# Two-layer hybrid decoder trunk: new order of the SBUF pools, slots of 2048 bytes, moving sides and weights 64 bytes apart modulo 128

## The chip, the core and the metric

The kernel runs on one core of a Trainium2 chip. The metric is the device time of one execution in microseconds (us), the median of three runs. The engines are named as in the profile: PE (matmuls), PEld (the weight loads of the same engine), DVE, ACT, POOL, and SP, whose queue issues nearly all DMAs.

## What is computed

The reference is a trunk of two layers over 256 positions of width 1024. Each layer has four token mixers that read one common projection, a gated merge, a SwiGLU of width 2816 and a gated side input; the rest is norms and residual adds. Nearly all of its arithmetic is products of a weight matrix with the activations:

```python
for i in range(DEPTH):                       # 2 layers
    u = _rmsnorm(h, norm_mix[i]) @ w_in[i]   # columns go to four mixers
    ...                                      # NSA, HGRN2, retention, RWKV-7, each to 256 columns
    merged = sum(sigmoid(x @ w_gate[i, m] + b_gate[i, m]) * (y[m] @ w_branch[i, m]) for m in range(4))
    h = h + merged @ w_out[i]
    x = _rmsnorm(h, norm_ffn[i])
    h = h + (silu(x @ w_ffn_gate[i]) * (x @ w_ffn_up[i])) @ w_ffn_down[i]
    x = _rmsnorm(h, norm_ple[i])
    h = h + sigmoid(x @ w_ple_gate[i]) * (p[i] @ w_ple_proj[i])
```

## The kernel before, in words

Activations stand feature-major: 128 partitions by 256 positions for each of the 8 pieces of the width. Every product is made in three matmuls of rounded fp32 ("fp32r"): weights and activations are each split into a rounded part (`hi`, tiles wh, xh) and the rest (`lo`, tiles wl, xl), and `mm3` (L221 to L223) adds wl·xh, wh·xl and wh·xh into one PSUM tile. The weights are the stationary side (128x128, loaded anew for each matmul), the activations the moving side (128x256). `gemm_pair` does the same where the last pieces of the activations come late (L256 to L258). `in_tm1` and `in_tm2` (L425 to L427) have the sides exchanged.

Weights come in tiles of 128x1024. `w_load` issues the DMA on SP into wr (4 buffers), ACT rounds it into wh (L206, 3 buffers), DVE or POOL subtracts into wl (L207, 3 buffers). One tile feeds 24 matmuls. A scheduler with priorities sets the order on each engine; small matmuls of the mixers (L141) are put between those of the big products.

The moving sides are: xh and xl, the normed activations (all of the projection, the gates, the SwiGLU's gate and up products); tiles A, T and Y made by `split` (L370, L371); U and M for the side input's gate. They come from the rotating tags A (18 buffers), B (13), U, T (6 each), Y0 to Y3 (2 each), M (4), which `t` and `g` take out of one pool.

SBUF is laid out by the pools in the order const, act, w, and inside a pool by first use. A tile's size in bytes for one partition is rounded up to 32. Some slots of A and U are larger than 2048 bytes (`rwkv_in` asks for T + 1 columns, 2056 bytes, `rwkv` for 65 where there are 64, `nsa_cmp` for 528), so their neighbours start at different places. The built program's addresses for one partition, modulo 128 (plain arithmetic on the layout, no times):

| tile | role | before | changed |
|---|---|---|---|
| wh, wl (all buffers; slices of a tile are 512 bytes apart) | weights | 64 | 64 |
| xh, xl (pieces are 1024 bytes apart) | moving | 64 | 0 |
| A | moving in the output and down products | 64, 96, 0, 32 in turn | 0 |
| U | moving in the side input's gate | 0 and 64 in turn | 0 |
| M | moving there, too | 64 | 0 |
| T | moving in the last pieces of the down product | 32 | 0 |
| Y0, Y3 | moving in two of the branch products | 0 | 0 |
| Y1, Y2 | moving in the other two, and for p | 32 | 0 |

`small` (vectors and small weights) is loaded into one tile for each layer, sm[0] and sm[1], both near the start. `rwkv` and `nsa_hid` read the small weights out of it.

Of the kernel before, what the change touches and what calls it, by code (L numbers as in the profile page):

```python
# [23 lines left out]
F32 = mybir.dt.float32  # L24
F32R = mybir.dt.float32r
BF = mybir.dt.bfloat16
I32 = mybir.dt.int32
AF = mybir.ActivationFunctionType
OP = mybir.AluOpType
# [3 lines left out]
P = 128  # L33
L = 2
T = 256
# [9 lines left out]
NV = 96  # L45

S_VEC = 0
S_WAU, S_GUP, S_K2, S_V2, S_PK, S_PV = (NV + x for x in (0, 256, 512, 640, 704, 720))
NS = S_PV + 16


C_ID, C_COS, C_SIN, C_DEC = 0, 128, 384, 640
# [98 lines left out]
class Trunk:  # L151
# [4 lines left out]

    def t(self, shape, tag, dt=F32, bufs=1):
        self.n += 1
        return self.act.tile(list(shape), dt, tag=tag, name=f"{tag}_{self.n}", bufs=bufs)

    def g(self, shape, stream=None, dt=F32):

# [8 lines left out]
    def run(self):  # L171
        tc = self.tc
        self.n = 0
        with (
            tc.tile_pool(name="const", bufs=1) as self.cst,
            tc.tile_pool(name="act", bufs=1) as self.act,
            tc.tile_pool(name="w", bufs=1) as self.wp,
            tc.tile_pool(name="ps", bufs=1, space=PS) as self.psp,
        ):
            self.body()  # L180
# [248 lines left out]
    def in_tm2(self, l):  # L429

        nc = self.nc
        ps = [self.ps([P, 512], "mm") for _ in range(2)]
        xs = self.xs()
        for g in range(2):
            hi, lo = self.w_load(self.ins["w_tm2"][l, g])
            for kk in range(4):
                k = 4 * g + kk
                s = slice(kk * 256, (kk + 1) * 256)
                for c in range(2):
                    ts = slice(c * P, (c + 1) * P)  # L440
                    self.mm3x(ps[c][:, :256], xs[k][0][:, ts], xs[k][1][:, ts], hi[:, s], lo[:, s], k == 0, k == 7)
        tm = self.t([P, 2, T], "tm2")
        for c in range(2):
            nc.vector.tensor_scalar(tm[:, c], ps[c][:, :256], self.rt[:, c:c + 1], 0.5, op0=OP.mult, op1=OP.mult)
        return tm
# [41 lines left out]
    def rwkv_in(self, l):  # L487
        nc = self.nc
        V = nc.vector
        v = lambda col: self.vec[l][:, col:col + 1]  # L490
        self.stream = "A"
        if l == 0:
            self.one_less_mu(l)
        ums = []
        for p in (3, 1, 0, 2):
            u = self.g([P, 2, T + 1])
            nc.gpsimd.memset(u[:, :, 0:1], 0.0)
            ps = self.in_pair(l, 2 * p, 2 if p == 3 else 0, "pA" if p in (3, 1) else "mm")
            mul = V.tensor_mul(u[:, :, 1:], ps, self.rstd_b)
            if p == 1:  # L500
                self.second = mul
            w = self.g([P, 2, T])
            um = self.g([P, 2, T])
            for c in range(2):
                i = 2 * p + c
                nc.scalar.activation(w[:, c], u[:, c, 1:], AF.Copy, scale=self.ommu[l][:, i:i + 1])
                V.scalar_tensor_tensor(um[:, c], u[:, c, :T], v(V_MU + i), w[:, c], op0=OP.mult, op1=OP.add)
            ums.append(um)
        return ums

    def rwkv(self, l, ums):
# [30 lines left out]
        V.tensor_tensor_scan(b.rearrange("p j t -> p (j t)"), self.reset, lw.rearrange("p j t -> p (j t)"), 0.0,  # L542
                             op0=OP.mult, op1=OP.add)
        b4 = b.rearrange("p j (c t) -> p j c t", c=4)
        pt = self.g([P, 2, 4, 65])
        nc.gpsimd.memset(pt[:, :, :, 0:1], 1.0)
        for j in range(2):
            nc.scalar.activation(pt[:, j, :, 1:], b4[:, j], AF.Exp)
# [354 lines left out]
    def nsa_in(self, l):  # L903
        nc = self.nc
        V = nc.vector
        sm = self.sm[l]
        rb = self.rstd
        lo, up = slice(0, 64), slice(64, 128)
        ps = self.in_pair(l, 16)
        kv = self.g([P, 16, 2, 16], "U")  # L910
        for i, src in ((0, lo), (1, up)):
            kb = kv[:, :, i].rearrange("p j n -> p n j")
            jn = lambda x: x.rearrange("p (n j) -> p n j", j=16)
            V.tensor_mul(kb[lo, :15], jn(ps[src, 0, :240]), jn(rb[src, :240]))
            V.tensor_mul(kb[up, :15], jn(ps[src, 0, 16:]), jn(rb[src, 16:]))
            V.tensor_copy(kv[:, :, i, 15], sm[:, S_PK + 16 * i:S_PK + 16 * i + 16])

        ksw = self.g([P, 528], "U")
        kx = ksw[:, 16:].rearrange("p (x b t) -> p b x t", x=2, b=2)
        xt = lambda a: a.rearrange("p (x t) -> p x t", x=2)  # L920
        for i, (src, dst) in enumerate(((lo, up), (up, lo))):
            V.tensor_mul(kx[src, i], xt(ps[src, 1]), xt(rb[src]))
            nc.scalar.activation(kx[dst, i], kx[src, i], AF.Copy)
        q = self.g([P, 2, T], "U")
        ps = self.in_pair(l, 14)
        V.scalar_tensor_tensor(q, ps, 0.125, self.rstd_b, op0=OP.mult, op1=OP.mult)
        return kv, ksw, q
# [138 lines left out]
    def setup(self):  # L1066
        nc, cst = self.nc, self.cst
        self.inv_dm = cst.tile([P, 1], F32, name="inv_dm")
        nc.vector.memset(self.inv_dm, 1.0 / DM)
        w = cst.tile([P, 1], F32, name="first")  # L1070
        nc.scalar.activation(w, self.inv_dm, AF.Copy)

        z = cst.tile([P, P], BF, name="zeros")
        nc.vector.memset(z, 0.0)
        ps = self.ps([P, P], "mm")
        for _ in range(72):
            nc.tensor.matmul(ps, z, z, start=True, stop=True)
        self.c = c = cst.tile([P, NC_], F32, name="cst")
        self.h = cst.tile([P, 8, T], F32, name="h")
        self.sm = [cst.tile([P, NS], F32, name=f"sm{l}") for l in range(L)]  # L1080
        nc.scalar.dma_start(self.sm[0][:, :NV], self.ins["small"][0][:, :NV])
        self.ahead = []
        for p in range(3):
            nc.sync.dma_start(self.h[:, 2 * p:2 * p + 2], self.ins["x"][:, 2 * p:2 * p + 2])
            if p == 0:
                self.ahead.append(self.w_tiles([self.ins["w_fm"][0, 6]], 2))
        nc.scalar.dma_start(c[:, :P], self.ins["consts"][:, :P])
        self.vec = [s[:, S_VEC:S_VEC + NV] for s in self.sm]
        self.xh = cst.tile([P, 8, T], F32R, name="xh")
        self.xl = cst.tile([P, 8, T], F32R, name="xl")  # L1090
        self.ident = c[:, C_ID:C_ID + P]
        self.ommu = [cst.tile([P, 8], F32, name=f"ommu{l}") for l in range(L)]

# [13 lines left out]
    def one_less_mu(self, l):  # L1107
        self.nc.vector.tensor_scalar(self.ommu[l], self.vec[l][:, V_MU:V_MU + 8], -1.0, 1.0, op0=OP.mult, op1=OP.add)

    def setup_late(self):  # L1110
        nc, cst, c = self.nc, self.cst, self.c
        with self.tc.issue_after(self.last_load.ins):
            nc.sync.dma_start(self.sm[0][:, NV:], self.ins["small"][0][:, NV:])
            nc.sync.dma_start(c[:, P:], self.ins["consts"][:, P:NC_])
            nc.sync.dma_start(self.sm[1], self.ins["small"][1])
        self.cos, self.sin = c[:, C_COS:C_COS + T], c[:, C_SIN:C_SIN + T]
        self.dec = c[:, C_DEC:C_DEC + 1024].rearrange("p (h b t) -> p h b t", h=4, b=2)
        self.rmask = c[:, C_RM:C_RM + 256]
# [123 lines left out]
    def layer(self, l):  # L1242
# [11 lines left out]
        with lane("A", "G"):  # L1254
            if l == 0:
                self.setup_late()
        with lane("A", "G"):
            self.tc.cur_priority += (30, 60)[l]
            y3 = self.rwkv(l, ums)
# [122 lines left out]
def layouts(i):  # L1382
# [5 lines left out]
    w = A["w_in"]  # L1388
# [24 lines left out]
    sm = np.zeros((L, P, NS), np.float32)  # L1413
    cv = lambda a: a.reshape(-1, P).T
    for l in range(L):
        sm[l, :64, S_WAU:S_WAU + 256] = A["rwkv_w_up"][l]
        sm[l, 64:, S_WAU:S_WAU + 256] = A["rwkv_a_up"][l]
        sm[l, :, S_GUP:S_GUP + 256] = A["rwkv_g_up"][l]
        sm[l, :, S_K2:S_K2 + 64] = A["nsa_cmp_k2"][l]
        sm[l, :, S_K2 + 64:S_K2 + 128] = A["nsa_cmp_k2"][l]  # L1420
        sm[l, :, S_V2:S_V2 + 64] = A["nsa_cmp_v2"][l]
        for col, n in ((S_PK, "nsa_pos_k"), (S_PV, "nsa_pos_v")):
            sm[l, :64, col:col + 16] = A[n][l, :16].T
            sm[l, 64:, col:col + 16] = A[n][l, 16:].T
        vcols = ((V_MIX, "norm_mix"), (V_FFN, "norm_ffn"), (V_PLE, "norm_ple"), (V_HN, "hgrn_norm"), (V_RG, "ret_norm_g"),
                 (V_RB, "ret_norm_b"), (V_MU, "rwkv_mu"), (V_W0, "rwkv_w0"), (V_A0, "rwkv_a0"), (V_KK, "rwkv_k_k"),
                 (V_KA, "rwkv_k_a"), (V_RK, "rwkv_r_k"), (V_NG, "rwkv_norm_g"), (V_NB, "rwkv_norm_b"), (V_BG, "b_gate"))
        for col, n in vcols:
            a = cv(A[n][l].reshape(-1))
            sm[l, :, S_VEC + col:S_VEC + col + a.shape[1]] = a  # L1430
        a = cv(A["hgrn_lb_logits"].reshape(-1))
        sm[l, :, S_VEC + V_LB:S_VEC + V_LB + 4] = a
        sm[l, :, S_VEC + V_NF:S_VEC + V_NF + 8] = cv(A["norm_final"])
# [20 lines left out]
```

## Time and profile before

| what | value |
|---|---|
| median of 3 runs | 1062.36 us (1062.13 to 1063.89) |
| the profiled execution: its time | 1062.78 us |
| the profiled execution: span of its instructions | 1060.1 us |
| mean granted TensorE clock | 0.993 |
| busy: PE / PEld / DVE / ACT / POOL | 98 / 95 / 70 / 51 / 22 % |
| DMA | 171.32 MB, 162 GB/s over the span |

A matmul's record is longer than its distance to the next: matmuls are pipelined, and the records overlap. What one matmul costs in a full stream is therefore read from start to start in the timeline, or as a window's length over the matmuls that start in it; the mean duration in a group's row is not that. The time lies 2.7 us above the span (launch and end), which the change does not touch.

### The profile page before, as it was taken

The page shows a single profiled execution, that of the slowest core. Times are in us where ns is not written, and L with a number is a line of the kernel's source. Part 1 is how long each engine was busy: PE and PEld are TensorE (multiplying, and loading weights), DVE is VectorE, ACT ScalarE, POOL GpSimd, SP SyncE. Part 2 cuts the span into 40 slices and gives each one's busy share as a digit, 9 for nine tenths or more (in the row PEclk, how much of TensorE's full clock was granted, in tenths as well). Part 3 has the DMA queues.
Part 4 walks back from the last instruction along what each step waited for, and adds up shares of the span by engine and source line. Part 5 has one row for each costly group of instructions (what it writes and reads, how often), then busy time and mean ns, then how long its engine had stood idle before and what let it go on. Part 6 is the DMA issues. An engine that isn't in the chain of part 4 may idle for free.

```text
span 1060.1 us, 22813 instructions
## 1 busy us (share of the span) xinstructions
PE 1042.2 (98%) x9520; PEld 1001.9 (95%) x9520; DVE 739.5 (70%) x1216; ACT 541.8 (51%) x863; POOL 238.4 (22%) x162
## 2 busy tenths in 40 slices
PE   8999999999999999999899999999999999999996
PEld 8989988899999999999899999888999999999996
DVE  6888968755676667554878989576567767665456
ACT  5644555555655454444555545555546554444444
POOL 0100000044442242232510000000544432232322
PEclk9999999999999999999999999999999999999997
DMA  8555323255665656666544553323665656666551
GB/s 294 198 183 160 94 91 117 78 162 178 191 187 174 195 181 182 183 184 191 170 146 127 177 174 95 110 81 100 180 193 176 189 170 185 196 177 192 174 183 49
DMA packets 50359, 171.32 MB, mean 162 GB/s; under 512 B 5713, under 2 KB 6481, under 8 KB 50129
## 3 DMA queue, kind: packets, MB, share of 16 engines
q1 hardware_dynamic: 49968, 169.76, 52.1%
q8 instruction: 74, 1.21, 0.5%
q14 instruction: 29, 0.23, 0.1%
q10 hardware_dynamic: 288, 0.11, 0.0%
HBM read 168.80 MB, written 1.05 MB: 160 GB/s over the span
## 4 chain that ended last, share of the span: by engine, by line
PE 87%; DVE 7%; ACT 2%; issue 2%; POOL 1%; DMA 1%; DVEq 0%; ACTq 0%; POOLq 0%
PE mm L221 21%; PE mm L223 21%; PE mm L222 21%; PE pB L141 6%; PE pA L141 5%; DVE wl L207 2%; PE pA L221 2%; PE pA L222 2%; PE pA L223 2%; PE pA L257 1%; PE pA L256 1%; PE pA L258 1%; ACT wh L206 1%; PE mm L427 1%; DVE T L1346 1%
## 5 line engine op out<-in xcount | busy, mean ns | idle before, releaser
L206 ACT ACTIVATE wh<-wr 128x1024 fp32r<-128x1024 f32 (+3 forms) x314 | 325.0, 1038 | 364.8 <-PE mm L223 243.3
L207 DVE TENSOR_TENSOR wl<-wr,wh 128x1024 fp32r<-128x1024 f32 (+3 forms) x259 | 326.5, 1262 | 146.8 <-ACT wh L206 143.8
L221 PE MATMUL mm<-xh,wl 128*128 128x256 f32 x1472 | 418.3, 284 | 0.5 <-POOL wl L207 0.5
L223 PE MATMUL mm<-xh,wh 128*128 128x256 f32 x1472 | 416.9, 283 | 0.0
L222 PE MATMUL mm<-xl,wh 128*128 128x256 f32 x1472 | 416.9, 283 | 0.0
L221 PEld LDWEIGHTS mm<-xh,wl 128*128 128x128 f32 x1472 | 277.1, 188 | 4.2 <-issue 1.6
L223 PEld LDWEIGHTS mm<-xh,wh 128*128 128x128 f32 x1472 | 277.1, 188 | 2.7 <-issue 1.5
L222 PEld LDWEIGHTS mm<-xl,wh 128*128 128x128 f32 x1472 | 277.1, 188 | 2.7 <-issue 1.5
L207 POOL TENSOR_TENSOR wl<-wr,wh 128x1024 fp32r<-128x1024 f32 (+1 forms) x55 | 130.1, 2367 | 274.9 <-ACT wh L206 274.9
L222 PE MATMUL mm<-A,wh 128*128 128x256 f32 x332 | 93.2, 281 | 0.0
L223 PE MATMUL mm<-A,wh 128*128 128x256 f32 x332 | 93.2, 281 | 0.0
L221 PE MATMUL mm<-A,wl 128*128 128x256 f32 x332 | 93.2, 281 | 0.0
L1325 POOL TENSOR_TENSOR B<-B,B 128x512 f32<-128x512 f32 x22 | 28.3, 1288 | 155.1 <-DVE B L1323 149.2
L223 PEld LDWEIGHTS mm<-A,wh 128*128 128x128 f32 x332 | 62.6, 189 | 0.0
L222 PEld LDWEIGHTS mm<-A,wh 128*128 128x128 f32 x332 | 62.6, 189 | 0.0
L221 PEld LDWEIGHTS mm<-A,wl 128*128 128x128 f32 x332 | 62.6, 189 | 0.0
L371 DVE TENSOR_TENSOR A<-B,A 128x512 fp32r<-128x512 f32 x18 | 36.6, 2033 | 33.2 <-ACT A L370 33.2
L141 PE MATMUL pA<-A,A 64*64 64x64 f32 (+3 forms) x1008 | 49.7, 223 | 0.3
L141 PEld LDWEIGHTS pA<-A,A 64*64 64x64 f32 (+3 forms) x1008 | 41.6, 135 | 8.3 <-issue 0.8
L221 PE MATMUL mm<-Y,wl 128*128 128x256 f32 x160 | 45.2, 282 | 0.0
L222 PE MATMUL mm<-Y,wh 128*128 128x256 f32 x160 | 45.0, 281 | 0.0
L223 PE MATMUL mm<-Y,wh 128*128 128x256 f32 x160 | 44.8, 280 | 0.0
(388 smaller groups left out, 1740.4 us busy)
## 6 DMA issues: line engine op xcount, KB each, us to landing
wr<-in_w_gate_dram SPq DMA_DIRECT2D x64, 512.0 KB, 3.7
wr<-in_w_fm_dram SPq DMA_DIRECT2D x46, 512.0 KB, 3.7
wr<-in_w_fg_dram SPq DMA_DIRECT2D x44, 512.0 KB, 4.4
wr<-in_w_fu_dram SPq DMA_DIRECT2D x44, 512.0 KB, 3.7
wr<-in_w_fd_dram SPq DMA_DIRECT2D x32, 512.0 KB, 4.2
wr<-in_w_branch_dram SPq DMA_DIRECT2D x16, 512.0 KB, 4.1
wr<-in_w_out_dram SPq DMA_DIRECT2D x16, 512.0 KB, 3.7
wr<-in_w_pg_dram SPq DMA_DIRECT2D x16, 512.0 KB, 4.4
```

The lines of the kernel that those rows point to most:

```text
L141: f(*args, **kw)
L206: nc.scalar.activation(hi[:, s], raw[:, s], AF.Copy)
L207: e.tensor_sub(lo[:, s], raw[:, s], hi[:, s])
L221: mm(out, wlo, xhi, start=start, stop=False)
L222: mm(out, whi, xlo, start=False, stop=False)
L223: mm(out, whi, xhi, start=False, stop=stop)
L256: mm(ps[:, c], lo, xs[k][0], start=c == 0 and k == 0, stop=False, skip_group_check=True)
L257: mm(ps[:, c], hi, xs[k][1], start=False, stop=False, skip_group_check=True)
L258: mm(ps[:, c], hi, xs[k][0], start=False, stop=k == n - 1, skip_group_check=True)
L371: self.nc.vector.tensor_sub(lo, src, hi)
L427: mm(out, xhi, whi, start=False, stop=stop)
L1325: G.tensor_mul(up, th, up)
```

## The change

The pools are opened in the order x, big, gap, w, const, act. All rotating tags go to `big`, whose slots are all exactly 2048 bytes; xh and xl stand ahead of it, and one tile of 64 bytes in `gap` stands between it and the weights. So every moving side starts at 0 modulo 128 and every weight slice at 64 (table above). In detail, for weights minus moving side modulo 512: 128 for xh and xl before, 192 for Y0 and Y3 before, 64 for all after.

The tiles larger than 2048 bytes leave these slots: the state table `pt` and `ksw` get tiles of their own, the projection `tm2` moves the other way, into a Y0 slot, and the token shift of `rwkv_in` is written without the extra column. That drops a memset on POOL for each of its four products, and the scaled copy goes straight into um (a tile less), whose columns from 1 on get the shifted term in place. The small weights of both layers share one buffer: layer 1's are loaded when layer 1 starts.

```diff
     def t(self, shape, tag, dt=F32, bufs=1):
-        return self.act.tile(list(shape), dt, tag=tag, name=f"{tag}_{self.n}", bufs=bufs)
+        pool = self.big if tag in BUFS else self.act
+        return pool.tile(list(shape), dt, tag=tag, name=f"{tag}_{self.n}", bufs=bufs)
...
+            tc.tile_pool(name="x", bufs=1) as self.xpool,
+            tc.tile_pool(name="big", bufs=1) as self.big,
+            tc.tile_pool(name="gap", bufs=1) as self.gap,
+            tc.tile_pool(name="w", bufs=1) as self.wp,
             tc.tile_pool(name="const", bufs=1) as self.cst,
             tc.tile_pool(name="act", bufs=1) as self.act,
-            tc.tile_pool(name="w", bufs=1) as self.wp,
...
-        tm = self.t([P, 2, T], "tm2")
+        tm = self.g([P, 2, T], "Y0")
...
-            u = self.g([P, 2, T + 1])
-            nc.gpsimd.memset(u[:, :, 0:1], 0.0)
+            u = self.g([P, 2, T])
...
-            mul = V.tensor_mul(u[:, :, 1:], ps, self.rstd_b)
+            mul = V.tensor_mul(u, ps, self.rstd_b)
...
-            w = self.g([P, 2, T])
             um = self.g([P, 2, T])
...
-                nc.scalar.activation(w[:, c], u[:, c, 1:], AF.Copy, scale=self.ommu[l][:, i:i + 1])
-                V.scalar_tensor_tensor(um[:, c], u[:, c, :T], v(V_MU + i), w[:, c], op0=OP.mult, op1=OP.add)
+                nc.scalar.activation(um[:, c], u[:, c], AF.Copy, scale=self.ommu[l][:, i:i + 1])
+                V.scalar_tensor_tensor(um[:, c, 1:], u[:, c, :T - 1], v(V_MU + i), um[:, c, 1:], op0=OP.mult, op1=OP.add)
...
-        pt = self.g([P, 2, 4, 65])
+        pt = self.t([P, 2, 4, 65], "rw_pt")
...
-        ksw = self.g([P, 528], "U")
+        ksw = self.t([P, 528], "ns_ksw")
...
-        w = cst.tile([P, 1], F32, name="first")
+        w = self.gap.tile([P, 16], F32, name="first")[:, :1]
...
-        self.xh = cst.tile([P, 8, T], F32R, name="xh")
-        self.xl = cst.tile([P, 8, T], F32R, name="xl")
+        self.xh = self.xpool.tile([P, 8, T], F32R, name="xh")
+        self.xl = self.xpool.tile([P, 8, T], F32R, name="xl")
...
+    def small(self, l):
+        sm = self.t([P, NS - NV], "sm")
+        self.nc.sync.dma_start(sm, self.ins["small"][l][:, NV:])
+        self.sm.append(sm)
...
-            nc.sync.dma_start(self.sm[0][:, NV:], self.ins["small"][0][:, NV:])
+            self.small(0)
             nc.sync.dma_start(c[:, P:], self.ins["consts"][:, P:NC_])
-            nc.sync.dma_start(self.sm[1], self.ins["small"][1])
+            nc.sync.dma_start(self.vec[1], self.ins["small"][1][:, :NV])
...
             if l == 0:
                 self.setup_late()
+            else:
+                with self.tc.issue_after(self.last_load.ins):
+                    self.small(l)
```

The order of the instructions stays nearly as it was. On SP one DMA is added at the start of layer 1. These are the changed kernel's rows there: the last three weight tiles of `rwkv_in`, the new load of the small weights (sm), and the first tiles of the rotary products.

```order
L210 DMA wr_6866<-in_w_fm_dram 128x1024
L210 DMA wr_6904<-in_w_fm_dram 128x1024
L210 DMA wr_6934<-in_w_fm_dram 128x1024
L1116 DMA sm_6970<-in_small_dram 128x736
L210 DMA wr_7526<-in_w_fm_dram 128x1024
L210 DMA wr_7556<-in_w_fm_dram 128x1024
```

Before, wr_6934's counterpart is followed at once by the rotary tiles. The new row stands behind the eighth and last weight tile of `rwkv_in`.

On ACT, at the end of `rwkv_in` in layer 1, the rows of before (A are the tiles u, w and um; ommu is one minus mu):

```order
L506 ACTIVATE A_6760<-A_6696,ommu_167 128x256 x2
L206 ACTIVATE wh_7531<-wr_7530 128x1024
L391 ACTIVATE U_7525<-U_7525 128x256
L506 ACTIVATE A_6830<-A_6766,ommu_167 128x256 x2
L206 ACTIVATE wh_7561<-wr_7560 128x1024
L506 ACTIVATE A_6900<-A_6836,ommu_167 128x256 x2
L206 ACTIVATE wh_7598<-wr_7597 128x1024
L506 ACTIVATE A_6970<-A_6906,ommu_167 128x256 x2
```

and the rows of the change:

```order
L509 ACTIVATE A_6761<-A_6698,ommu_176 128x256 x2
L211 ACTIVATE wh_7527<-wr_7526 128x1024
L396 ACTIVATE U_7521<-U_7521 128x256
L509 ACTIVATE A_6829<-A_6766,ommu_176 128x256 x2
L211 ACTIVATE wh_7557<-wr_7556 128x1024
L509 ACTIVATE A_6897<-A_6834,ommu_176 128x256 x2
L211 ACTIVATE wh_7594<-wr_7593 128x1024
L509 ACTIVATE A_6965<-A_6902,ommu_176 128x256 x2
```

The rows stand in the same order; only the tile written differs (um in place of w).

## Rows read from the trace of the kernel before

**Rows 1.** The page: span, busy time and share of each engine, instructions.

```profile
span 1060.1 us, 22813 instructions
## 1 busy us (share of the span) xinstructions
PE 1042.2 (98%) x9520; PEld 1001.9 (95%) x9520; DVE 739.5 (70%) x1216; ACT 541.8 (51%) x863; POOL 238.4 (22%) x162
```

**Rows 2.** Windows of SwiGLU stages: length, busy of PE to POOL, clock, DMA.

```profile
300.00:425.00 125.00, 125.00 (x1057) 125.00 (x1056) 86.68 (x91) 61.94 (x74) 42.97 (x24) 1.00 0.60 184
820.00:945.00 125.00, 125.00 (x1057) 125.00 (x1056) 86.57 (x92) 62.31 (x74) 42.95 (x24) 1.00 0.61 185
425.00:490.00 65.00, 65.00 (x552) 65.00 (x551) 34.16 (x34) 30.98 (x37) 18.97 (x11) 1.00 0.63 187
945.00:1010.00 65.00, 65.00 (x553) 65.00 (x552) 35.24 (x35) 30.18 (x37) 17.63 (x10) 1.00 0.63 183
```

**Rows 3.** Groups by form: matmuls with moving sides xh, A, Y.

```profile
L221 PE MATMUL mm<-xh,wl 128*128 128x256 f32 x1472 | 418.3, 284 | 0.5 <-POOL wl L207 0.5
...
L222 PE MATMUL mm<-A,wh 128*128 128x256 f32 x332 | 93.2, 281 | 0.0
...
L221 PE MATMUL mm<-Y,wl 128*128 128x256 f32 x160 | 45.2, 282 | 0.0
...
L256 PE MATMUL pA<-xh,wl 128*128 128x256 f32 x64 | 18.9, 296 | 3.3 <-ACT xh L310 1.9 <-DVE wl L207 1.4
...
L221 PE MATMUL pA<-xh,wl 128*128 128x256 f32 x64 | 18.3, 286 | 1.2 <-DVE wl L207 1.2
```

**Rows 4.** Timeline of PE, branch products on Y3 and Y0: start, us, form.

```profile
248.77 0.28 PE L221 MATMUL mm<-Y,wl 128*128 128x256 f32 x1
...
254.31 0.28 PE L223 MATMUL mm<-Y,wh 128*128 128x256 f32 x1
...
770.21 0.28 PE L221 MATMUL mm<-Y,wl 128*128 128x256 f32 x1
...
775.74 0.28 PE L223 MATMUL mm<-Y,wh 128*128 128x256 f32 x1
...
799.14 0.28 PE L221 MATMUL mm<-Y,wl 128*128 128x256 f32 x1
...
804.79 0.28 PE L221 MATMUL mm<-Y,wl 128*128 128x256 f32 x1
```

**Rows 5.** DMA issues of the small weights: KB, us to landing.

```profile
sm<-in_small_dram SPq DMA_DIRECT2D x1, 416.0 KB, 7.5
sm<-in_small_dram SPq DMA_DIRECT2D x1, 368.0 KB, 4.7
```

**Rows 6.** Timeline at the start of layer 1: SP's weight loads, PE's first use of sm.

```profile
541.05 5.85 SPq L205 DMA_DIRECT2D wr<-in_w_fm_dram  x4
...
561.76 0.93 PE L141 MATMUL pA<-A,sm 64*128 64x256 f32 x6
```

**Rows 7.** Line L507, the shifted term: ns min/median/max, first and last start, who waited.

```profile
L507 DVE SCALAR_TENSOR_TENSOR A<-A,sm,A x16: 465/478/726, 27.4 to 558.7; 128x256 f32<-128x256 f32 x16
...
who waited for it (us, times):
  POOL A L546: 16.5, 2
```

**Rows 8.** PE's waits over the span: in total, times, longest.

```profile
PE pB L354 <- DVE rs_y2B L294: 2.5, 2, 1.9
PE pA L256 <- ACT xh L310: 1.9, 1, 1.9
PE pA L256 <- DVE wl L207: 1.4, 2, 0.7
```

**Rows 9.** Timeline of PE in the down product of layer 1, at 965 and 996 us.

```profile
965.01 0.29 PE L222 MATMUL mm<-A,wh 128*128 128x256 f32 x1
965.14 0.28 PE L223 MATMUL mm<-A,wh 128*128 128x256 f32 x1
965.26 0.28 PE L221 MATMUL mm<-A,wl 128*128 128x256 f32 x1
...
996.13 0.29 PE L222 MATMUL mm<-A,wh 128*128 128x256 f32 x1
996.26 0.28 PE L223 MATMUL mm<-A,wh 128*128 128x256 f32 x1
```

More of the change, by code (lines that the diff above doesn't have):

```diff
@@ L47 @@
 S_VEC = 0
-S_WAU, S_GUP, S_K2, S_V2, S_PK, S_PV = (NV + x for x in (0, 256, 512, 640, 704, 720))
-NS = S_PV + 16
+S_WAU, S_GUP, S_K2, S_V2, S_PK, S_PV = 0, 256, 512, 640, 704, 720
+NS = NV + S_PV + 16
 C_ID, C_COS, C_SIN, C_DEC = 0, 128, 384, 640
@@ L1079, in setup @@
         self.h = cst.tile([P, 8, T], F32, name="h")
-        self.sm = [cst.tile([P, NS], F32, name=f"sm{l}") for l in range(L)]
-        nc.scalar.dma_start(self.sm[0][:, :NV], self.ins["small"][0][:, :NV])
+        self.vec = [cst.tile([P, NV], F32, name=f"vec{l}") for l in range(L)]
+        self.sm = []
+        nc.scalar.dma_start(self.vec[0], self.ins["small"][0][:, :NV])
         self.ahead = []
@@ L1087, in setup @@
         nc.scalar.dma_start(c[:, :P], self.ins["consts"][:, :P])
-        self.vec = [s[:, S_VEC:S_VEC + NV] for s in self.sm]
-        self.xh = cst.tile([P, 8, T], F32R, name="xh")
-        self.xl = cst.tile([P, 8, T], F32R, name="xl")
+        self.xh = self.xpool.tile([P, 8, T], F32R, name="xh")
+        self.xl = self.xpool.tile([P, 8, T], F32R, name="xl")
         self.ident = c[:, C_ID:C_ID + P]
@@ L1415, in layouts @@
     for l in range(L):
[L1416 to L1421, printed above, removed]
+        sw = sm[l, :, NV:]
+        sw[:64, S_WAU:S_WAU + 256] = A["rwkv_w_up"][l]
+        sw[64:, S_WAU:S_WAU + 256] = A["rwkv_a_up"][l]
+        sw[:, S_GUP:S_GUP + 256] = A["rwkv_g_up"][l]
+        sw[:, S_K2:S_K2 + 64] = A["nsa_cmp_k2"][l]
+        sw[:, S_K2 + 64:S_K2 + 128] = A["nsa_cmp_k2"][l]
+        sw[:, S_V2:S_V2 + 64] = A["nsa_cmp_v2"][l]
         for col, n in ((S_PK, "nsa_pos_k"), (S_PV, "nsa_pos_v")):
-            sm[l, :64, col:col + 16] = A[n][l, :16].T
-            sm[l, 64:, col:col + 16] = A[n][l, 16:].T
+            sw[:64, col:col + 16] = A[n][l, :16].T
+            sw[64:, col:col + 16] = A[n][l, 16:].T
         vcols = ((V_MIX, "norm_mix"), (V_FFN, "norm_ffn"), (V_PLE, "norm_ple"), (V_HN, "hgrn_norm"), (V_RG, "ret_norm_g"),
```

## Prediction

> **What bounds the kernel now.** I read the page's busy times first. PE is busy for 98% of the span, its weight loads for 95%, DVE for 70% and ACT for 51% [rows 1]; what PE waits for by name is 2.5 us at most in one place [rows 8]. So the time is a stream of matmuls, and the question is how far apart they start. The mean of a group (284 ns for a matmul with moving side xh [rows 3]) does not say that, since the records overlap: 1472 matmuls of one line alone give 418.3 us of "busy" time, and there are three such lines.
>
> The windows say it [rows 2]. In the two SwiGLU stages with gate and up products PE is never idle, the clock is at its full level (1.00, that is 2.4 GHz), and 1057 matmuls have records in 125 us. A record of 0.28 us that began ahead of the window counts too, some 2.4 of them, so that 1054.6 start in it: 125 / 1054.6 = 118.5 ns from start to start. Nearly all of these have moving sides in xh and xl, at the same place modulo 128 as the weights (table in the section on the change). The same reading of the down product, where the moving sides stand at 64, 96, 0 and 32, gives 65 / 549.6 = 118.3 ns in layer 0 and 65 / 550.6 = 118.1 ns in layer 1.
>
> Before the change, there is one place in which every moving side is already 64 away from the weights: the branch products on Y3 and Y0, four runs of 48 matmuls. Three of them have rows [rows 4]: 248.77 to 254.31 are 47 distances, 117.9 ns each; 770.21 to 775.74 are 47, 117.7 ns; 799.14 to 804.79 are 48, 117.7 ns. I take 117.75 ns (two decimals in us make each of them good to about 0.2 ns). This is the trace's own sample of the changed layout, and it stands beside DVE, ACT, POOL and DMA work like any other stage.
>
> **The change part by part.** *The addresses.* 118.5 - 117.75 = 0.75 ns for a matmul whose moving side now stands at the weights' place. The xh and xl products are (1472 + 64 + 64) x 3 = 4800 matmuls [rows 3], which gives 4800 x 0.75 ns = 3.6 us. The other products, apart from the branches: the down product has 1056 matmuls, the output product 384 and the side input's gate 384 (its sides U and M stand at 0 or 64). With the mean of the down stages, 118.2 ns, they give (1056 + 384 + 384) x 0.45 ns = 0.8 us. Branch products gain nothing on Y3 and Y0 and too little to count on Y1 and Y2. All of this lies on the path, because PE has no gaps in these windows [rows 2]. Sum: 4.4 us.
>
> Both ends of this price: at the low end nothing, if the 0.75 ns belong to something else than addresses; below nothing is possible, too (last rival). At the high end a matmul cannot beat its 256 columns at the full clock, 106.7 ns, so that 11.8 ns for each of some 7200 matmuls would be 85 us. I take the value of the Y runs because nothing else in the trace has the same layout, and 47 distances in a row agree within the reading.
>
> *The small mixers' matmuls* (A with A, at 64x64) had mixed places and now have one. They are 64 columns long and alternate with waits for other engines; I put them at nothing, covered by the products that the scheduler puts between them.
>
> *The token shift.* Eight memsets on POOL go, and a tile. POOL is busy for 22% [rows 1]. ACT still makes 16 copies and DVE 16 shifted terms, of 255 columns in place of 256: 478 ns x 1/256 x 16 = 0.03 us less of DVE [rows 7]. The shifted term now reads and writes the same tile, which adds no wait, as it waited for the same copy before. Behind it, only POOL waits (16.5 us in two waits [rows 7]), for work that is not on the path. Nothing.
>
> *The load of sm.* Early, 416 KB shrink to 48 KB on SP; the load took 7.5 us to land [rows 5], but PE's waits of the whole run hold no weight DMA among the longest [rows 8], so nothing is won. At the start of layer 1, 368 KB are added behind the last weight tile of `rwkv_in`. It lands in 4.7 us by its twin in layer 0 [rows 5]. On SP the four weight loads around it go out between 541.05 and 546.9 us, and PE first reads sm at 561.76 [rows 6]: 15 us or more lie between, three landings' worth. Queued behind it are the rotary tiles, whose buffers (4 in wr) hold 4 x 24 x 118.5 ns = 11.4 us of matmuls; a load that comes 4.7 us later is still covered. The single buffer adds no wait, since layer 0 reads it last in its mixers, a whole SwiGLU before layer 1 starts. If this cover were gone, it would cost 4.7 us once; I put it at nothing.
>
> *tm2 in a Y0 slot.* The slot is next wanted when `nsa` splits its result, after `hgrn` has used tm2. Nothing.
>
> So the forecast is 1062.4 - 4.4 = 1058.0 us. The profiled execution took 1062.78 us, 0.4 us above the median, so that the same sum there gives 1058.4 us and a span of about 1055.7 us. Its own range is 1053 to 1060.2: 0.75 ns taken as 0.4 to 1.3 ns.
>
> **The rivals.** *No change, 1060.2 to 1064.5 us.* The Y runs could be even for another reason: short, with two tiles that lie next to each other. For it speaks that the difference is 0.6% and the down product, where only part of the sides stand badly, is hardly faster than the gate and up products (118.1 and 118.3 against 118.5 ns). Against it: four stages agree in the order that the addresses give. The Trainium skill has a rule that points this way: "TensorE: Matmul & The Clock Gate", Part 2, "Step-by-step", has two independent SBUF read ports for PE, one for the moving side and one for weights, so that loading the next weights takes nothing from the running matmul; by that alone no address could matter and the time would stay at 1062.4. The rows of the down product (below, 0.13 us in one fixed pair) speak against its strict form. This case also holds that the change does not do what it says, if modulo 128 is not what counts.
>
> *Far faster, under 1053 us.* If the part above 106.7 ns were all a clash of the two reads and went, the time would be 1062 - 85 = 977 us; a third of it would give 1034 us. Against it stand the Y runs, in which the sides are 64 apart already and 11 ns remain. By the skill's same page, section "Back-to-back issue gap", a warm matmul of 256 columns would be 256/2.4 + 2.5 = 109.2 ns, an estimate that would give 8.6 ns x 7200 = 62 us less; the Y runs' 117.75 ns disagree with it.
>
> *Slower, above 1064.5 us.* The offset within more than 128 bytes may count. Weights minus moving side is 192 modulo 512 in the Y runs, but 64 everywhere after the change. The trace shows that single pairs of tiles can cost more: in the down product one L222 matmul takes 0.13 us to the next where its neighbours take 0.12, at the same pair in every chunk (965.01 to 965.14, 996.13 to 996.26 [rows 9]). Its moving side stands at 64 modulo 512 from the weights, which is the new relation. If every third matmul (the L222) took those 8.5 ns more, that would be 2400 x 8.5 ns = 20 us, and 1083 us. It decides from a distance of 118.9 ns on, where the loss passes 2 us. Against it: other matmuls with the same relation take 0.12 us, and the costly pair also changes its place between two matmuls, which the new layout never does.
>
> **How the numbers follow.** Forecast 0.53, no change 0.27, far faster 0.06, slower 0.14. A measurement of this kernel can tell about 0.2%, 2.1 us, from no change, so that the forecast's own range ends there. Faster: nearly all of the forecast and the far faster case, with a little of "no change" to spare, 0.60. Same: 0.27. Slower: 0.13. The range, 1053 to 1064.5, takes in the forecast and "no change" and leaves out the far faster and the slower case, 0.2 together.
>
> **What would show it.** In the window of gate and up products: 117.75 ns, some 1064 records in 125 us in place of 1057, and the down product the same. Distances in a timeline of xh matmuls would be even, as in the Y runs. The page should show PE at 98% still, the sm load landed well before its first use, and no new wait of PE. The forecast is wrong if the stream keeps 118.5 ns, or if it goes under 117 ns, and then the Y runs were no sample of the layout. If the stream gets faster and the time does not, a wait at a stage's edge took it.

## The result, and the profile after

| | before | after |
|---|---|---|
| median of 4 runs on one chip | 1062.39 us | 1049.41 us (1047.52 to 1050.96) |
| ratio after / before | | 0.9874 [0.9854, 0.9894] |
| profiled execution: time, span | 1062.78, 1060.1 us | 1048.63, 1046.9 us |

The change makes the kernel 13.0 us (1.3%) faster. The direction was forecast; the size is three times the forecast (4.4 us) and lies outside the range. In the two profiled executions 13.2 us of the difference lie in the span; the time stands 2.7 us above the span before and 1.7 us after. The first part of the page of after, beside [rows 1], shows the same kernel with a shorter time of PE and its weight loads, and little else:

```profile
span 1046.9 us, 22801 instructions
## 1 busy us (share of the span) xinstructions
PE 1026.3 (98%) x9520; PEld 986.2 (94%) x9520; DVE 738.5 (71%) x1216; ACT 542.9 (52%) x863; POOL 240.2 (23%) x154
```

PE's busy time falls by 15.9 us for the same 9520 matmuls, that of its weight loads by 15.7 us; DVE, ACT and POOL differ from before by 1 to 2 us. The 8 instructions that POOL lost are the memsets.

The windows of the two SwiGLU stages (columns as in [rows 2]; 4 us earlier in layer 0, 10 us earlier in layer 1, since the work comes earlier):

```profile
296.00:421.00 125.00, 125.00 (x1069) 125.00 (x1067) 87.06 (x92) 63.01 (x74) 43.19 (x24) 1.00 0.62 187
810.00:935.00 125.00, 125.00 (x1069) 125.00 (x1068) 87.15 (x91) 62.96 (x74) 43.24 (x24) 1.00 0.61 188
421.00:486.00 65.00, 65.00 (x554) 65.00 (x553) 34.64 (x34) 30.87 (x37) 19.40 (x11) 1.00 0.61 184
935.00:1000.00 65.00, 65.00 (x554) 65.00 (x553) 35.27 (x34) 30.23 (x37) 19.39 (x11) 1.00 0.62 187
```

With 2.4 straddling records taken off, the first two go from 118.5 to 125 / 1066.6 = 117.2 ns, the last two to 65 / 551.6 = 117.8 ns. These windows are not pure, though: the first starts some 11 us before the SwiGLU, in the output product (moving side A, about a tenth of its matmuls), the third ahead of the down product. A window that lies wholly in the gate and up products, first of before, then of after:

```profile
330.00:400.00 70.00, 70.00 (x592) 70.00 (x591) 48.52 (x46) 34.35 (x38) 23.15 (x13) 1.00 0.60 183
330.00:400.00 70.00, 70.00 (x596) 70.00 (x596) 47.59 (x44) 34.01 (x37) 22.17 (x13) 1.00 0.62 187
```

That is 70 / (592 - 2.4) = 118.7 ns before and 70 / (596 - 2.4) = 117.9 ns after: nearly what was forecast for these products, and it can't give 13 us. The gain is elsewhere. A window inside the gates stage, first of before, then of after:

```profile
223.00:248.00 25.00, 25.00 (x213) 25.00 (x212) 13.47 (x13) 12.03 (x15) 12.99 (x7) 1.00 0.59 171
```

```profile
223.00:248.00 25.00, 25.00 (x223) 25.00 (x223) 13.81 (x15) 12.79 (x17) 11.87 (x6) 1.00 0.69 202
```

25 / (213 - 2.4) = 118.7 ns there becomes 25 / (223 - 2.4) = 113.3 ns, at the same granted clock of 1.00. The timeline of PE in after shows that these are two ways in which one and the same stream can run. First in the gates stage, then in the SwiGLU, both on xh and xl:

```profile
240.83 0.28 PE L228 MATMUL mm<-xh,wh 128*128 128x256 f32 x1
...
241.85 0.28 PE L228 MATMUL mm<-xh,wh 128*128 128x256 f32 x1
...
360.93 0.28 PE L228 MATMUL mm<-xh,wh 128*128 128x256 f32 x1
...
361.99 0.28 PE L228 MATMUL mm<-xh,wh 128*128 128x256 f32 x1
```

Nine distances take 1.02 us in the first piece (113 ns each) and 1.06 us in the second (118 ns each). Measured over hundreds of matmuls from their start times, the two values are **113.3 ns** and **117.8 ns**. In after a stream takes one of them and keeps it until something breaks it: a wait of PE, or a small matmul between the large ones. I call them the short and the long distance. Before the change neither exists for xh and xl: single distances scatter from 115 to 122 ns around 118.7.

Where the 13 us come from, by comparing the start of the matmul with the same number in both traces:

| matmuls | stage | layer 0 | layer 1 |
|---|---|---|---|
| 0 to 1999, 5600 to 6799 | projection and mixers | -1.7 us | -1.1 us |
| 2000 to 3199, 6800 to 7999 | gates, branches, output product, start of SwiGLU | -3.6 | -3.6 |
| 3200 to 4799, 8000 to 9199 | rest of SwiGLU with the down product | -1.1 | -0.7 |
| 4800 to 5599, 9200 to the end | side input, and the next layer's start | -0.7 | -0.7 |

The stages with short distances give 3 ns a matmul (3.6 us by 1200), the rest of the SwiGLU 0.6 to 0.7 ns. In after, all of the SwiGLU from its second pair of chunks on, down product included, is one unbroken stream of 1424 matmuls (1423 distances) in each layer, and in the profiled execution both had the long distance.

The last sample is the one that the forecast stood on. The same branch products on Y as in [rows 4], in after:

```profile
245.37 0.28 PE L226 MATMUL mm<-Y,wl 128*128 128x256 f32 x1
...
250.69 0.28 PE L228 MATMUL mm<-Y,wh 128*128 128x256 f32 x1
```

47 distances in 5.32 us are 113.2 ns, where before had 117.9 ns with the sides already 64 apart modulo 128. What changed for them is weights minus moving side modulo 512: 192 before, 64 after.

### The profile page after: what moved, and what is told of

It reads as the page before. It is cut to its first block, busy times and chain, and to the rows that moved or that the text cites. A ratio compares the mean times of both kernels' runs of the same rounds, so it can differ in the third digit from the quotient of the medians.

```text
span 1046.9 us, 22801 instructions
## 1 busy us (share of the span) xinstructions
PE 1026.3 (98%) x9520; PEld 986.2 (94%) x9520; DVE 738.5 (71%) x1216; ACT 542.9 (52%) x863; POOL 240.2 (23%) x154
## 4 chain that ended last, share of the span: by engine, by line
PE 85%; DVE 9%; ACT 2%; issue 2%; DMA 1%; POOL 1%; DVEq 0%; ACTq 0%; POOLq 0%
PE mm L226 21%; PE mm L227 21%; PE mm L228 21%; PE pB L141 6%; PE pA L141 5%; DVE wl L212 3%; PE pA L226 2%; PE pA L227 2%; PE pA L228 2%; PE pA L262 1%; PE pA L261 1%; PE pA L263 1%; DMA T<-in_w_cmp_dram 1%; ACT wh L211 1%; DVE T L1358 1%
## 5 line engine op out<-in xcount | busy, mean ns | idle before, releaser
L1249 POOL TENSOR_TENSOR M<-M,T 128x512 f32<-128x512 f32 x24 | 43.4, 1839 | 9.9 <-DVE T L1248 9.9
L227 PE MATMUL mm<-Y,wh 128*128 128x256 f32 x160 | 44.4, 278 | 0.0
```

The source lines that it names most:

```text
L227: mm(out, whi, xlo, start=False, stop=False)
L1249: self.nc.gpsimd.tensor_add(merged[p], merged[p], ths[p])
```

## The experiments

Three theories. **A:** moving side and weights 64 apart modulo 128 make the stream settle into one of two fixed distances, and only this pays. **B:** something else in the change pays (equal slots, the order of pools, the side edits). **C:** the place inside 512 bytes counts. A', in the later runs: which of the two distances a stream has is drawn anew at each break. The kernels named gapN are the changed kernel with the gap tile set so that weights minus moving side is N modulo 512 (gap576: 576 bytes of gap, 64 modulo 512 again). "Streams" below are runs of at least 24 large matmuls (128x256, full array) with no start more than 150 ns behind the one before. A stream is short or long when its last 16 distances have a mean within 0.6 ns of 113.3 or of 117.8 ns and a standard deviation under 1 ns; the others are of neither kind. Each count is from one profiled execution. The changed kernel has 34 short, 17 long and no other.

| kernel | weights minus moving | median us (lowest to highest) | ratio to before, interval | streams short : long |
|---|---|---|---|---|
| gap128 | 128 | 1063.43 (1061.61 to 1064.63) | 1.0006 [0.9997, 1.0016] | neither |
| gap32 | 32 | 1061.1 (1059.4 to 1062.97) | 0.9987 [0.9978, 0.9996] | neither |
| gap96 | 96 | 1061.76 (1060.1 to 1062.88) | 0.9989 [0.9978, 1.0] | neither |
| gap192 | 192 | 1056.57 (1054.86 to 1056.85) | 0.9942 [0.9927, 0.9957] | 6 : 44 |
| gap448 | 448 | 1056.19 (1055.21 to 1058.16) | 0.9945 [0.993, 0.996] | 4 : 45 |
| gap576 | 64 | 1049.5 (1037.7 to 1050.04) | 0.9854 [0.9801, 0.9906] | 28 : 22 |
| gap320 | 320 | 1043.3 (1037.53 to 1049.12) | 0.9822 [0.9772, 0.9871] | 29 : 22 |
| xonly | 64 for xh, xl alone | 1052.3 (1051.69 to 1054.16) | 0.9908 [0.9893, 0.9923] | 24 : 11, 14 of neither kind |

### The gap made to 128 bytes: all of the change but the offset

```diff
-        w = self.gap.tile([P, 16], F32, name="first")[:, :1]
+        w = self.gap.tile([P, 32], F32, name="first")[:, :1]
```

> The changed kernel with the gap tile grown from 64 to 128 bytes: all slots, the order of the pools and every other edit stay, but weights and moving sides stand at the same place modulo 128. Theory A (64 bytes apart modulo 128 lets the stream settle into one of two fixed distances, 113.3 or 117.8 ns): no stretch settles at 113.3 ns, distances scatter around 118.6 ns as before, and the time is back at 1060 to 1064 us. Theory B (the gain comes from equal slots or from the small edits, not from the 64 bytes): 1047 to 1051 us, as the changed kernel.

Measured 1063.43 us: the gain is gone. A window of the SwiGLU in this kernel:

```profile
330.00:400.00 70.00, 70.00 (x592) 70.00 (x591) 48.51 (x46) 33.94 (x38) 23.15 (x13) 1.00 0.61 182
```

70 / (592 - 2.4) = 118.7 ns, and no stream with either fixed distance. This kernel has the pools, the slots of 2048 bytes and every side edit. B falls: these are worth nothing that the noise would let one see, and 64 bytes of gap are worth 13 us.

### The kernel before, with xh and xl alone moved by 64 bytes

```diff
+        self.ommu = [cst.tile([P, 8], F32, name=f"ommu{l}") for l in range(L)]
         self.xh = cst.tile([P, 8, T], F32R, name="xh")
...
-        self.ommu = [cst.tile([P, 8], F32, name=f"ommu{l}") for l in range(L)]
```

> The kernel before with one edit: the two small tiles ommu are allocated ahead of xh and xl, which moves xh and xl by 64 bytes and nothing else, so that these (4800 of 7200 matmuls) stand 64 from the weights, and A, T, U, M, Y where they stood. Theory A: gates and SwiGLU gate and up products settle at 113.3 or 117.8 ns; the down and output products stay at 118.2; about two thirds of the gain, 1052 to 1057 us. Theory B: 1061 to 1064 us.

Measured 1052.3 us, 10 of the 13 us, by moving one allocation ahead of another. This is A again from the other side. Here the weights and all else stay where they stood, while the gap runs leave xh and xl and move the weights; so it is the place of the one against the other that counts, and not the place of either. The rest is in the products whose sides stay mixed here. By start-to-start times in the two traces, after is ahead of xonly by 2.4 us on Y (the branches), 2.4 us on A (mostly the output product) and 1.1 us on U and M, and 0.9 us behind it on xh and xl.

This trace shows one thing more. In the gates stage xh and xl run at the long distance ahead of a run of Y and at the short one behind it, with neither a wait nor a small matmul in between:

```profile
216.14 0.28 PE L221 MATMUL mm<-xh,wl 128*128 128x256 f32 x1
...
217.20 0.28 PE L221 MATMUL mm<-xh,wl 128*128 128x256 f32 x1
...
230.10 0.28 PE L221 MATMUL mm<-xh,wl 128*128 128x256 f32 x1
...
231.12 0.28 PE L221 MATMUL mm<-xh,wl 128*128 128x256 f32 x1
```

Nine distances take 1.06 us, then 1.02 us. So a stretch of sides that stand otherwise acts as a break, too.

### The gap made to 192 bytes: 64 modulo 128, but 192 modulo 512

```diff
-        w = self.gap.tile([P, 16], F32, name="first")[:, :1]
+        w = self.gap.tile([P, 48], F32, name="first")[:, :1]
```

> The changed kernel with a gap tile of 192 bytes: weights minus moving side is 192 modulo 512 in place of 64, and still 64 modulo 128. Theory A (modulo 128 alone counts): the same two distances, 113.3 and 117.8 ns, and 1044 to 1054 us, according to which of the two the long SwiGLU stretches get. Theory C (the offset inside 512 bytes counts): other distances, 1056 to 1064 us, like the 117.8 ns of the runs on Y before.

Measured 1056.57 us, some 6 us less than before and not 13. A window of the SwiGLU, and the branch products on Y:

```profile
330.00:400.00 70.00, 70.00 (x596) 70.00 (x596) 49.02 (x46) 34.61 (x40) 22.91 (x13) 1.00 0.62 183
```

```profile
247.53 0.28 PE L226 MATMUL mm<-Y,wl 128*128 128x256 f32 x1
...
253.06 0.28 PE L228 MATMUL mm<-Y,wh 128*128 128x256 f32 x1
```

The SwiGLU has 117.9 ns; the Y run is back at 5.53 / 47 = 117.7 ns, as in [rows 4]. The same two distances occur as in after (A), but 44 of 50 streams take the long one. So the half of 128 bytes makes the two distances, and the place inside 512 goes with how often each is taken: C holds for the share, not for the distances. This is where the forecast went wrong.

### The gap made to 32 and to 96 bytes

```diff
-        w = self.gap.tile([P, 16], F32, name="first")[:, :1]
+        w = self.gap.tile([P, 8], F32, name="first")[:, :1]
```

(with 24 in place of 8 for 96 bytes)

> The changed kernel with a gap tile of 32 bytes: all weights 32 from all moving sides modulo 128. Theory A says 64 is the best place; at 32 part of the clash is left, and distances lie between 113.3 and 118.6 ns: 1050 to 1062 us. Theory B: 1047 to 1051 us.

> The changed kernel with weights 96 bytes behind the moving sides modulo 128. Theory A (64 is a place of its own): scattered distances around 118 ns as at 32, 1057 to 1063 us. If any distance of 64 or more did it: 1047 to 1053 us.

Measured 1061.1 and 1061.76 us. The SwiGLU of gap32, then of gap96:

```profile
330.00:400.00 70.00, 70.00 (x594) 70.00 (x593) 48.64 (x46) 35.11 (x39) 23.23 (x13) 1.00 0.62 184
330.00:400.00 70.00, 70.00 (x593) 70.00 (x592) 48.56 (x46) 34.54 (x38) 23.20 (x13) 1.00 0.60 183
```

118.3 and, over the whole stretch, 118.7 ns, scattered, without a fixed distance. A quarter of 128 bytes gives about a tenth of the gain that the half gives with 32 bytes (1.5 us), and with 96 bytes a time that can't be told from no change (0.7 us, the interval ends at 1.0).

### The gap made to 320, 448 and 576 bytes

```diff
-        w = self.gap.tile([P, 16], F32, name="first")[:, :1]
+        w = self.gap.tile([P, 80], F32, name="first")[:, :1]
```

(112 and 144 for the other two)

> The changed kernel with a gap tile of 320 bytes: weights minus moving side is 320 modulo 512, 64 modulo 128. Theory A: two distances, 113.3 and 117.8 ns; the share of each may differ from the changed kernel's as it did at 192: 1040 to 1057 us. Theory C' (of the four places 64 apart, only 64 modulo 512 gives many stretches at 113.3 ns): 1055 to 1058 us, as at 192.

> As the run with 320, at 448 modulo 512. Theory A: two distances, 1040 to 1057 us. Theory C': 1055 to 1058 us. If 256 is the period of what selects, 320 goes with 64 (1049) and 448 with 192 (1056.5).

> The changed kernel with a gap tile of 576 bytes: the same 64 modulo 512, but 512 bytes further. If 512 bytes (one weight slice) is the period of what counts: the changed kernel's time and the same stretches, 1047 to 1051 us. If longer offsets count too, or the share of the two distances is chance: another share, anywhere in 1040 to 1057 us.

448 does what 192 does, and 320 has about as many short streams as 64: as far as these kernels and one trace of each go, the share repeats after 256 bytes, and C' falls. With 320 and 576, single executions fall on levels 6 us apart: 1037.53, then 1043.27 and 1043.34, then 1049.12 us for gap320; 1037.7, then 1049.16 to 1050.04 us for gap576. The profiled execution of gap320 (1043.27 us) shows why, in two windows at the middle of the SwiGLU of layer 0 and of layer 1:

```profile
330.00:400.00 70.00, 70.00 (x620) 70.00 (x619) 47.99 (x46) 35.09 (x40) 23.96 (x14) 1.00 0.63 194
850.00:920.00 70.00, 70.00 (x597) 70.00 (x596) 47.38 (x43) 33.70 (x37) 21.97 (x12) 1.00 0.61 190
```

70 / (620 - 2.4) = 113.3 ns in layer 0, 117.7 ns in layer 1: the same code, the same addresses, the same execution. One long stretch is worth 1423 x 4.45 ns = 6.3 us, which is the step between the levels. What a long stretch gets differs by layer and, as the times say, by execution. Four runs are few for such a spread: that gap320's median lies below that of after may be the luck of the draw (gap576, at the very offset of after, fell on the lowest level once, too).

### Breaks put into the stream

A matmul of bf16 zeros (full 128 weight columns, 8 to 128 columns long) is added into the up product of nine pairs in each layer. It adds nothing to the sum.

```diff
                 self.mm3(out, hi[:, s], lo[:, s], xs[k][0], xs[k][1], k == 0, k == len(xs) - 1)
+                if kick and k == 1:
+                    self.nc.tensor.matmul(out[:, :kick], self.z, self.z[:, :kick], start=False, stop=False,
+                                          skip_group_check=True)
```

> The changed kernel with one more matmul in the up product of pairs 2 to 10 of each SwiGLU: bf16 zeros times zeros, 8 to 128 columns, added to the running sum (adds nothing to it). It breaks the stream once in each pair. Theory A' (which of the two distances a stretch gets is drawn anew at each break and then kept): after some of the 18 breaks the stream goes on at 113.3 ns, after others at 117.8 ns, and each holds to the next break; 4.5 ns x 48 matmuls or 0.2 us less for each pair at 113.3, less about 0.1 us for each break: 1046 to 1051 us. Theory D (the SwiGLU's distance belongs to its addresses or its neighbours on other engines, not to the break): 117.8 ns after every break, 1049 to 1052 us.

One execution, 1049.94 us. The timeline of PE at the break of 371.76 us:

```profile
370.35 0.28 PE L229 MATMUL mm<-xh,wl 128*128 128x256 f32 x1
...
371.64 0.28 PE L231 MATMUL mm<-xh,wh 128*128 128x256 f32 x1
371.76 0.20 PE L249 MATMUL mm<-zeros 128*128 128x64 bf16 x1
371.80 0.36 PE L229 MATMUL mm<-xh,wl 128*128 128x256 f32 x1
372.00 0.28 PE L230 MATMUL mm<-xl,wh 128*128 128x256 f32 x1
...
372.92 0.28 PE L229 MATMUL mm<-xh,wl 128*128 128x256 f32 x1
```

Ahead of it, 11 distances in 1.29 us (117 ns). Behind it the first takes 0.20 us, and then 8 take 0.92 us (115 ns: the first of them are still long, the last ones 0.113). From there to the next break the mean is 113.34 ns. Of the 18 breaks 4 met the short distance, and all 4 led to the long one; 14 met the long one, and 4 of them led to the short one. The two breaks with 64 columns both led to the short distance, the other 16 in two cases (16 and 128 columns); that is too few to tell whether the column count matters. So breaks draw the distance, and between them it holds (A').

### One break of another kind, ahead of the long stretch

In after, the first full step behind a break is longer than the others. Where it takes 0.20 us, mostly the long distance follows; where it takes 0.22 to 0.23 us, which mostly stands behind matmuls on half the array or less (64 weight columns or rows), mostly the short one. Over the streams of after, gap576 and gap320: 16 short to 41 long behind the first, 72 to 13 behind the second. So one zero matmul with 64 weight columns was put into each layer, in the up product of pair 1, just ahead of the long stretch; likewise in gap320 (kick320) and in gap128 (kick128).

```diff
+KICKS = ({1: 64}, {1: 64})
...
+                if kick and k == 1:
+                    self.nc.tensor.matmul(out[:64, :kick], self.z[:, :64], self.z[:, :kick], start=False, stop=False,
+                                          tile_position=(0, 0), skip_group_check=True)
```

> The changed kernel with one more matmul in each layer: bf16 zeros of 64 weight columns (half the array) and 64 moving columns, added to the running sum of the up product of pair 1, just ahead of the long unbroken stretch (about 1420 matmuls). In the changed kernel's trace, most streams that start behind such a half-array matmul settle at 113.3 ns. Theory A' (the break sets which distance the stretch keeps): both long stretches at 113.3 ns in most executions, 2 x 1420 x 4.5 ns = 12.8 us less, 1035 to 1044 us. Theory D (the SwiGLU's distance belongs to its place, not to the break): 117.8 ns as now, 1047 to 1052 us.

> The same extra matmul on the run with a gap tile of 320 bytes, whose executions fell on 1037.5, 1043.3 and 1049.1 us. Theory A': the long stretches of both layers at 113.3 ns nearly always, 1034 to 1042 us, with less spread. Theory D: 1037 to 1050 us spread as before.

> The same extra matmul on the run with weights and moving sides at the same place modulo 128. Theory A (only 64 bytes apart are there two fixed distances to choose from): no stretch at 113.3 ns, 1060 to 1065 us. If the break alone gave the fast stream, whatever the addresses: 1047 to 1055 us.

| kernel | median us (lowest to highest) | ratio to before, interval |
|---|---|---|
| kick | 1037.39 (1036.79 to 1038.34) | 0.9763 [0.9748, 0.9778] |
| kick320 | 1038.27 (1036.97 to 1039.02) | 0.9769 [0.9753, 0.9785] |
| kick128 | 1063.44 (1061.99 to 1064.19) | 1.0007 [0.9998, 1.0017] |

kick beats both kernels: 25.1 us less than before, 12.0 less than after; two stretches of some 1390 matmuls by 4.45 ns are 12.4 us. The break in its timeline, and the windows that answer to those of after:

```profile
326.62 0.22 PE L249 MATMUL mm<-zeros 128*64 128x64 bf16 x1
326.77 0.38 PE L229 MATMUL mm<-xh,wl 128*128 128x256 f32 x1
327.00 0.28 PE L230 MATMUL mm<-xl,wh 128*128 128x256 f32 x1
```

```profile
290.00:415.00 125.00, 125.00 (x1098) 124.83 (x1097) 88.73 (x95) 65.81 (x79) 43.93 (x25) 1.00 0.62 191
800.00:925.00 125.00, 125.00 (x1098) 124.83 (x1097) 89.74 (x96) 65.97 (x79) 43.06 (x24) 1.00 0.63 190
415.00:480.00 65.00, 65.00 (x576) 65.00 (x575) 36.51 (x36) 31.66 (x38) 20.02 (x11) 1.00 0.65 197
```

1098 records in 125 us, where after has 1069 and before 1057; in the down product 65 / 573.6 = 113.3 ns. The spread over levels is gone in kick320 as well (1036.97 to 1039.02 us where gap320 had 1037.53 to 1049.12); D falls. Against the first set of breaks, the kind (half the array in place of all), the place (pair 1) and, against most of them, the number of columns (now 64 in both layers) changed together, and no run separates them. kick128 shows that the break by itself gives nothing: without the offset there are no two distances to choose from.

## Why the prediction was wrong

*PE's stream as the bound, and the direction:* right. All of the gain is PE's, and no other engine became the bound.

*The 0.75 ns for a matmul on xh and xl:* this term failed, and with it the step "I take the value of the Y runs because nothing else in the trace has the same layout". Their 117.75 ns was the long one of two distances. At 192 and 448 modulo 512 nearly every stream takes the long one (gap192 44 of 50, gap448 45 of 49), so that four even runs could easily miss the other. At 64 more than half of the streams are short, and a matmul there gains 118.7 - 113.3 = 5.4 ns in place of 0.75. Over all xh and xl products the mean distance in the traces falls from 118.6 to 116.1 ns, 2.6 ns by 4665 distances, or 12 us where 3.6 us stood in the sum. The forecast said itself that the Y runs stand at 192 and the change at 64, and took that difference for a risk only.

*The high end of that price* (106.7 ns) was in the text, but the range didn't go there. The far faster rival, under 1053 us, is the case that came true, though not by its mechanism: not a part of the 11 ns everywhere, but 5 ns in some streams.

*The readings of the windows:* the window from 300 us holds the output product up to 312 us, and the one from 425 us gate and up products up to 439 us. So "nearly all" is 89% of the matmuls, and gate and up products alone stood at 118.7 ns, not 118.5. This makes the term 0.2 ns larger, and does not explain the miss.

*Nothing for the branches, 0.45 ns for the other products:* the branch products on Y were put at nothing and fell from 118.1 to 113.9 ns on average, 2 us in all; most of the output product runs at 113.3 ns. The down product came to 117.8 ns, 0.3 to 0.5 less than before, as forecast. It lies in the long stretch, so that it, too, could have had 113.3 ns, as kick shows.

*The slower rival* (the place within 512 costs a pair of tiles, [rows 9]): right that the place counts, wrong in sign. 64 is the better relation, and in the long stretches of after no distance is above 119 ns.

*The no change rival:* refuted. The Trainium skill, "TensorE: Matmul & The Clock Gate", Part 2, "Step-by-step", gives PE two independent SBUF read ports. 64 bytes of gap change the time by 14 us (1063.43 against 1049.41), so in this kernel the place of one side against the other does matter; whether the two reads are what meets there, no run shows. The Trainium skill, same page, section "Back-to-back issue gap", has 256/2.4 + 2.5 = 109.2 ns for a warm matmul taken by itself, an estimate from its formula. No offset tried here reaches it: the best stream has 113.3 ns.

*The edits put at nothing:* right, as gap128 shows for all of them together. For the load of sm in layer 1, SP's queue in after:

```profile
526.78 8.42 SPq L210 DMA_DIRECT2D wr<-in_w_fm_dram  x2
535.25 0.43 SPq L1116 DMA_DIRECT2D sm<-in_small_dram  x1
536.08 13.58 SPq L210 DMA_DIRECT2D wr<-in_w_fm_dram  x6
```

and the summary of the matmuls that read sm in layer 1, with first and last start:

```profile
L141 PE MATMUL pA<-A,sm x12: 376/377/480, 555.2 to 559.4; 64*128 64x256 f32 x8, 128*128 128x256 f32 x4
```

It is issued at 535.25 and takes 4.8 us at most; PE first reads it at 555.2, and no wait of PE names it. The longest waits of PE are of the same kinds as in [rows 8], and 2.6 us at most in total:

```profile
PE pB L359 <- DVE rs_y2B L299: 2.6, 2, 1.9
PE pA L261 <- ACT xh L315: 2.5, 1, 2.5
```

*What would show it:* the window was forecast at 1064 records and has 1069; the excess is from the output product at its head, which runs at the short distance. The text's own alarm, a stream under 117 ns, went off in the gates stage.

Open: why the distances are 113.3 and 117.8 ns, why 192 and 448 rarely give the short one, and why the half-array break leads to it more often than the full one. That PE's reads of the two sides meet in SBUF would fit, but it is argued from the addresses alone; no counter in the trace shows it.

## What to carry to other kernels

All of this is measured in one kernel. Where a profile shows PE full and its matmuls of this form 118 ns apart or more, look at the addresses: place weights and moving sides 64 bytes apart modulo 128, and try 64 or 320 modulo 512 before 192 or 448. Then read the distances from start to start by stage, not as one mean; if a long stretch sits at the long one, a tiny matmul at its head can move it, as in all 8 runs of kick and kick320. A window that is to stand for one product must lie wholly in it. And a sample from the trace of before bounds a new layout only if it agrees in everything that the layout changes.

## What was unexpected of the hardware

With weights and moving sides 64 bytes apart modulo 128, a stream of rounded fp32 matmuls of 256 columns, with a weight load for each, has two stable distances, 113.3 and 117.8 ns, at one and the same granted clock (1.00) and in one and the same code. It holds either for more than 1400 matmuls (160 us), and the choice differs between executions: 1037.5 to 1049.1 us for one kernel. One zero matmul in each layer, of 64 columns, took 12 us off the time.
